# One engine for the branch stage's two-operand steps, and running sums for the pooling means

## The chip, the core and the metric

The kernel runs on one core of a Trainium2 chip. A core has five engines that each work through their own queue of instructions in order: TensorE (PE in the profile; its weight loads are PEld), VectorE (DVE), ScalarE (ACT), GpSimd (POOL) and SyncE (SP), which here issues the loads and stores. TensorE writes to PSUM, in banks; all else lies in SBUF. The metric is the device time of one execution, in microseconds (us).

## The reference

One layer of a decoder trunk on 16 learned meta tokens and 1024 input tokens (L = 1040), width 1024. All is float32.

```
u = rmsnorm(h)
q, f, i, g, v_pool, gate_a, gate_b = split(u @ w_in)
a = hgrn2(q, f, i, g)            # 4 heads of 128: gated linear recurrence, decay per channel
p = multiscale_pool(v_pool)      # 4 groups of 128 channels, windows 2, 4, 8, 16
z = sigmoid(gate_a) * (a @ w_branch_hgrn) + sigmoid(gate_b) * (p @ w_branch_pool)
h = h + rmsnorm(z @ w_out)
u = rmsnorm(h)
y = (gelu(causal_conv3(u @ w_gate)) * (u @ w_up)) @ w_down
out = (h + rmsnorm(y))[16:]
```

The pooling of a group with window w is the mean of the last w values less the value itself, then a 128 x 128 projection:

```
cs0 = cumsum(v, time), with a zero in front
outs = (cs0[t+1] - cs0[t+1-w]) / min(t+1, w) - v[t]
```

In the recurrence, b is the running sum of log f within a chunk, and a pair of times t > s contributes q_t exp(b_t - b_s) k_s.

## The kernel before, in words

Every float32 matrix product is made of three products: each operand is split in a rounded first part and the rest (`hi`, `lo`), and hi x hi, hi x lo and lo x hi are summed. The split of a weight tile (`wsplit`, lines 132 to 139) is a load, a copy on ScalarE that rounds (line 137) and a subtraction that makes the second part (line 138).

The work lies in stages along time: the norm and the value projection, the gates' products (a Strassen scheme), the **branch stage**, the output projection with norms, and the MLP. The branch stage runs from about 285 to 580 us of the profile. It has 34 jobs of projections (F, Q, G, PV, PP, BB, BA: forget logits, queries, output gates, pooling values, pooling projections and the two branch outputs), and between them the steps of the four heads (`h`), the rest of the forget gate (`c`) and the splits of the pooled values and of the heads' outputs (`sp`, `sa`). The list ORDER, line 45, gives the order in which all these are written down. The engines' own order within this stage is not written by hand: a planner, which simulates the engines with a cost model when the kernel is compiled, lays out each engine's queue, in the main by that order. The stages after it have their order fixed for TensorE, ScalarE, VectorE and mostly GpSimd.

A head's steps (`head_steps`, line 578):

- Six levels, of block lengths 2 to 64, taken in three pairs. For each, `level_in` subtracts from b its value at the middle of each block (line 597), takes two exponentials on ScalarE (lines 599, 600) and multiplies one half of every block by q (line 601) and the other by k (line 602), each product over 512 or 520 columns. TensorE makes the small products (lines 613, 619), and VectorE copies them into the scores (lines 633 to 640).
- The decays to the end of a chunk and from its start (lines 654 to 664), a factor on every second q and k (lines 667 to 674), transposes, the states of the eight chunks (line 716), and the output with its norm and gate (lines 725 to 746).

`chain_f` (line 562) makes log f and its running sum b with a scan (line 569). `post_pv` (line 764) copies a pooling group's values from PSUM to `vp` on ScalarE and sums each window by doubling: one addition of shifted copies for window 2, up to four for window 16, all on GpSimd (line 776). `pool_split` (line 780) overwrites the sum of the first kept time for window 16, scales, subtracts `vp` (line 788) and splits the result (lines 793, 794).

Which engine takes a two-operand step is said by the list POOLED: a step named in it goes to GpSimd, all others to VectorE. For example lq8.1 is line 601 of level 8 and head 1, wPV2 the second part of the weights of the job PV2. All tiles of this stage are slots of one ring of 24.

Of the kernel before, what the change touches and what calls it, by code (L numbers as in the profile page):

```python
# [12 lines left out]
ALU = mybir.AluOpType  # L13

P = 128
# [3 lines left out]
L = SEQ + NM  # L19
# [25 lines left out]
ORDER = ("F0 c0 Q0 h0 F1 h0 c1 Q1 h0 h1 F2 h1 c2 h0 Q2 h1 h2 G2 h0 h1 h2 h0 F3 h0 h2 c3 PV0 h1 h2 h1 Q3 h3 h1 "  # L45
         "h3 h1 PV1 h3 sp0 PV2 h2 h3 sa1 sp1 sp2 PP0 h2 PV3 h2 h3 sp3 PP1 h0 G3 h3 PP2 h3 PP3 BB0 h2 BB1 BB2 "
         "sa2 BB3 h3 BB4 BB5 sa0 sa3 BA0 BA1 BB6 BA2 BB7 BA3 BA4 BA5 BA6 BA7")
POOLED = ("e1k.0 e1k.3 kdmul.2 kdmul.3 kdsub.2 lk32.1 lk4.1 lk64.0 lq16.1 lq16.3 lq32.0 lq32.1 lq32.2 lq4.0 "
          "lq64.0 lq64.3 lq8.0 lq8.1 lq8.2 osg.2 qsmul.2 qsmul.3 sub2.2 sub32.1 sub4.1 sub8.1 sub8.3 wBA2 wBA6 "
          "wBA7 wBB2 wF0 wF2 wF3 wPP2 wPV0 wPV1 wPV2 wPV3 wQ0 wQ1 wQ3").split()  # L50
TRUNC = False

CH_ALL = [(0, 348), (348, 346), (694, 346)]
# [4 lines left out]
def trunk_kernel(ctx: ExitStack, tc: tile.TileContext, x, meta_tokens, mix_norm_pre,  # L58
# [4 lines left out]
    act, dve, pool_e, pe = nc.scalar, nc.vector, nc.gpsimd, nc.tensor  # L63
# [21 lines left out]
    def nm(s):  # L85
        cnt[0] += 1
        return f"{s}_{cnt[0]}"

    def slot(n, dtype=F32, name="s"):
        return stage["fm", "p"].tile([P, n], dtype, tag="fm", name=nm(name), padded_shape=[P, L])  # L90
# [65 lines left out]
    def wblock(w, k0, n_k, c0, n_c):  # L156
        return w[k0 * P : (k0 + n_k) * P, c0 : c0 + n_c].rearrange("(k p) c -> p k c", p=P)
# [387 lines left out]
    def blocks(t, lo, h):  # L545
        return t[:, lo:L].rearrange("p (b two h) -> p b two h", two=2, h=h)

    heads = [dict() for _ in range(HEADS)]

    def eng(op):  # L550
        return pool_e if op in POOLED else dve

    sgs = {}

    def post_f(h, pf):
        kk, b, f, f2 = slot(L, name="kk"), slot(L, name="b"), slot(L, name="f"), slot(L, name="f2")
        for (lo, n), ps in zip(CH_ALL, pf):
            act.activation(f[:, lo : lo + n], ps[:, :n], AF.Sigmoid)
            act.activation(kk[:, lo : lo + n], ps[:, :n], AF.Sigmoid, scale=-1.0)
        return lambda: chain_f(h, kk, b, f, f2)  # L560

    def chain_f(h, kk, b, f, f2):
        dve.tensor_scalar(f, f, oml[:, h : h + 1], lb[:, h : h + 1], ALU.mult, ALU.add)
        dve.tensor_scalar(f2, f, LOG_FLOOR, LSPLIT, ALU.max, ALU.min)
        dve.tensor_scalar(f, f, LSPLIT, None, ALU.max)
        act.activation(f2, f2, AF.Ln, scale=LUP)
        act.activation(f, f, AF.Ln)
        eng(f"lf.{h}").tensor_tensor(f, f, f2, ALU.add)
        dve.tensor_tensor_scan(b, again, f, 0.0, ALU.mult, ALU.add)
        heads[h].update(kk=kk, b=b, f=f)  # L570

    def post_q(h, pq):
        q = slot(L, name="q")
        for (lo, n), ps in zip(CH_ALL, pq):
            act.activation(q[:, lo : lo + n], ps[:, :n], AF.Copy, scale=oml[:, h : h + 1])
        heads[h]["q"] = q

    def head_steps(h):
        q, kk, b, lf = (heads[h][z] for z in ("q", "kk", "b", "f"))
# [11 lines left out]
        def level_in(lv):  # L591
            lo = 0 if 2 * lv <= NM else NM
            nb = (L - lo) // (2 * lv)
            d = slot(L, name="d")
            bb, db = blocks(b, lo, lv), blocks(d, lo, lv)
            mid = bb[:, :, 0, lv - 1 : lv]
            eng(f"sub{lv}.{h}").tensor_tensor(db.rearrange("p b two h -> p b (two h)"), bb.rearrange("p b two h -> p b (two h)"),
                              mid.to_broadcast([P, nb, 2 * lv]), ALU.subtract)
            act.activation(db[:, :, 1, :], db[:, :, 1, :], AF.Exp)
            act.activation(db[:, :, 0, :], db[:, :, 0, :], AF.Exp, scale=-1.0)  # L600
            eng(f"lq{lv}.{h}").tensor_tensor(db[:, :, 1, :], db[:, :, 1, :], blocks(q, lo, lv)[:, :, 1, :], ALU.mult)
            eng(f"lk{lv}.{h}").tensor_tensor(db[:, :, 0, :], db[:, :, 0, :], blocks(kk, lo, lv)[:, :, 0, :], ALU.mult)
            return d

        def level_mm(lv, qk):
# [47 lines left out]
        qs, kd = slot(L, name="qs"), slot(L, name="kd")  # L653
        act.activation(qs, b, AF.Exp)
        for t0, n, w in ((0, 1, NM), (NM, NCH, P)):
            bc = b[:, t0 : t0 + n * w].rearrange("p (c t) -> p c t", t=w)
            kc = kd[:, t0 : t0 + n * w].rearrange("p (c t) -> p c t", t=w)
            eng(f"kdsub.{h}").tensor_tensor(kc, bc[:, :, w - 1 : w].to_broadcast([P, n, w]), bc, ALU.subtract)
        act.activation(kd, kd, AF.Exp)
        ebl = small([P, NCH], "ebl", "ebl", 2)  # L660
        act.activation(ebl.rearrange("p (c t) -> p c t", t=1),
                       b[:, NM:L].rearrange("p (c t) -> p c t", t=P)[:, :, P - 1 : P], AF.Exp)
        eng(f"kdmul.{h}").tensor_tensor(kd, kd, kk, ALU.mult)
        eng(f"qsmul.{h}").tensor_tensor(qs, qs, q, ALU.mult)


        e1 = slot(L, name="e1")
# [2 lines left out]
        act.activation(e1[:, L // 2 :], lo2, AF.Exp, scale=-1.0)  # L670
        q2 = q.rearrange("p (b two) -> p b two", two=2)[:, :, 1]
        k2 = kk.rearrange("p (b two) -> p b two", two=2)[:, :, 1]
        eng(f"e1q.{h}").tensor_tensor(q2, q2, e1[:, : L // 2], ALU.mult)
        eng(f"e1k.{h}").tensor_tensor(k2, k2, e1[:, L // 2 :], ALU.mult)
        yield
        kt = slot(NCH * P, name="kt")
        for j in range(2):
# [43 lines left out]
        o, rs = slot(TQ, name="o"), slot(TQ, name="rs")  # L721
# [21 lines left out]
        act.activation(rs, rs, AF.Exp, scale=-0.5)  # L743
        dve.scalar_tensor_tensor(o, o, ong[:, h : h + 1], rs, ALU.mult, ALU.mult)
        sg = sgs[h]
        eng(f"osg.{h}").tensor_tensor(o, o, sg, ALU.mult)
        heads[h] = dict(o=o)

    sgd = dram.tile([EARLY_G, P, TQ], F32, name="gscr")
# [1 line left out]
    def post_g(h, pg):  # L751
        sg = slot(TQ, name="sg")
        for (lo, n), ps in zip(CH_Q, pg):
            act.activation(sg[:, lo : lo + n], ps[:, :n], AF.Sigmoid)
        if h < EARLY_G:
            nc.sync.dma_start(sgd[h], sg)
        else:
            sgs[h] = sg
# [4 lines left out]

    def post_pv(g, pv):
        w = POOL_WINDOWS[g]
        vp, s1 = slot(L, name="vp"), slot(L, name="s1")
        s2 = slot(L, name="s2") if w > 2 else None
        for (lo, n), ps in zip(CH_ALL, pv):
            act.copy(vp[:, lo : lo + n], ps[:, :n])
        cur, step = vp, 1  # L770
        bufs = [s1, s2]
        while step < w:
            nxt = bufs[0]
            bufs = bufs[::-1]
            a = 2 * step - 1
            pool_e.tensor_tensor(nxt[:, a:L], cur[:, a:L], cur[:, a - step : L - step], ALU.add)
            cur, step = nxt, 2 * step
        pooled[g] = (cur, vp)

    def pool_split(g):  # L780
# [16 lines left out]
    def post_pp(g, pp):  # L797
        a, b_ = slot(TQ, F32R, "phi"), slot(TQ, F32R, "plo")
        for (lo, n), ps in zip(CH_Q, pp):
            act.activation(a[:, lo : lo + n], ps[:, :n], AF.Copy, scale=psc[:, g : g + 1])  # L800
            dve.scalar_tensor_tensor(b_[:, lo : lo + n], ps[:, :n], psc[:, g : g + 1], rr(a[:, lo : lo + n]),
                                     ALU.mult, ALU.subtract)
        phi[g], plo[g] = a, b_
# [21 lines left out]
    def post_branch(d, m, qa):  # L825
        for (lo, n), ps in zip(CH_Q, qa):
            dve.tensor_tensor(d[m][:, lo : lo + n], d[m][:, lo : lo + n], ps[:, :n], ALU.mult)
# [11 lines left out]
    def job(kind, i):  # L839
        if kind == "F":  # L840
            return (wblock(WIN, 0, KD, CF + i * P, P), KD, u_all, CH_ALL, lambda r: post_f(i, r))
        if kind == "Q":
            return (wblock(WIN, 0, KD, CQ + i * P, P), KD, u_all, CH_ALL, lambda r: post_q(i, r))
        if kind == "G":
            return (wblock(WIN, 0, KD, CG + i * P, P), KD, u_q, CH_Q, lambda r: post_g(i, r))
        if kind == "PV":
            return (wblock(WIN, 0, KD, CV + i * P, P), KD, u_all, CH_ALL, lambda r: post_pv(i, r))
        if kind == "PP":
            return (pool_proj[0, i].rearrange("(k c) d -> c k d", k=1), 1,
                    lambda k, lo, n: (pin[i][0][:, lo : lo + n], pin[i][1][:, lo : lo + n]), CH_Q,  # L850
                    lambda r: post_pp(i, r))
        if kind == "BA":
            return (wblock(w_branch_hgrn[0], 0, HEADS, i * P, P), HEADS, a_x, CH_Q, lambda r: post_branch(sas, i, r))
        return (wblock(w_branch_pool[0], 0, HEADS, i * P, P), HEADS, p_x, CH_Q, lambda r: post_branch(sbs, i, r))

    order = ORDER.split()
    order = [(o_[:-1], int(o_[-1])) for o_ in order]
# [40 lines left out]
    with tc.manual_schedule(engines={E.Activation, E.DVE, E.PE}):  # L898
# [75 lines left out]
        for e in range(0, EARLY, 2):  # L974
            p = gates.start_pair(e)
# [5 lines left out]
    close_pool("pf")  # L981
    open_pool("ps", 8, PSUM)

    loader = Loader([job(*o_)[:2] + (P, eng("w%s%d" % o_)) for o_ in order if o_[0].isupper()])

    def split_z(c, k):
        zc = slot(2 * CW, F32R, "zc")
# [331 lines left out]
    with tc.manual_schedule(engines={E.PE, E.Activation, E.DVE, E.Pool}):  # L1319
        for c in range(3):  # L1320
            tiles_ = [pair("pm") for _ in range(3)]
            own = Rows(c, tiles_)
            for k in range(KD if c < 2 else KD - 3):
                w = wo.next()
# [45 lines left out]
        p = [ffn.first(e) for e in range(EARLY)]  # L1370
# [171 lines left out]
```

## Time and profile before

| | |
|---|---|
| median of 3 runs | 1375.14 us (1374.52 to 1375.27) |
| the profiled execution | 1376.13 us, its span 1374.4 us |
| granted TensorE clock, mean | 0.991 |
| TensorE busy | 1330.5 us, 97% of the span |
| VectorE busy | 945.2 us, 69% |
| ScalarE busy | 572.9 us, 42% |
| GpSimd busy | 478.8 us, 35% |

The profile records one execution. A busy share is an average over all stages, so a stage is read by itself: the busy time of each engine in a stretch, who waited for whom in it, and the single instructions. In a row of a group of instructions stand the line, the engine, the operation, output and input tiles with their shapes, the count, the busy time in us, the mean duration in ns, and the idle time of the engine in front of them with what ended it. Tile names are those of the program: `d` a level's operand, `sl` its products, `kd` and `qs` the decays, `s` and `vp` the pooling, `whi` and `wlo` the two parts of a weight, `wraw` the weight as it was loaded.

### The profile page before, as it was taken

What the parts mean: (1) busy time and instruction counts of PE and PEld (TensorE: products, weight loads), DVE (VectorE), ACT (ScalarE), POOL (GpSimd) and SP (SyncE); (2) the same over time, 40 slices, a digit from 0 to 9 for tenths busy, and PEclk for the clock granted to TensorE, in tenths of its full rate; (3) what the DMA queues carried; (4) which work ended last, traced back from release to release, by engine and by line L of the source; (5) the groups of instructions that cost most, each with busy time, mean ns of one, the idle gap of its engine ahead of it and who ended that gap; (6) DMA issues with size and microseconds to landing.
All of it is one profiled execution on the core that took longest, in us unless ns stands there. A gap on an engine that the chain in (4) does not pass through costs nothing. (4 is left out here: it accounts for less than half of the span.)

```text
span 1374.4 us, 23322 instructions
## 1 busy us (share of the span) xinstructions
PE 1330.5 (97%) x9375; PEld 1201.1 (87%) x9375; DVE 945.2 (69%) x1213; ACT 572.9 (42%) x965; POOL 478.8 (35%) x371
## 2 busy tenths in 40 slices
PE   9999999998999899999988999999999999999997
PEld 6899999998999899977677888988899998788786
DVE  6764544379877654655689898887888776744557
ACT  5553333366666552135654222232222223643334
POOL 4015421236545410250047565454557642000100
PEclk9999999999999999999999999999999999999999
DMA  7135332311110043698833677756677799965514
GB/s 248 39 101 161 116 112 96 116 48 47 50 50 6 24 139 108 211 291 312 290 116 91 190 209 200 193 175 164 155 162 168 180 233 259 381 218 196 183 62 168
DMA packets 133227, 215.34 MB, mean 157 GB/s; under 512 B 8327, under 2 KB 76523, under 8 KB 133120
## 3 DMA queue, kind: packets, MB, share of 16 engines
q1 hardware_dynamic: 121056, 189.47, 41.4%
q0 software_dynamic: 12064, 24.38, 10.5%
q8 instruction: 74, 1.21, 0.4%
q14 instruction: 33, 0.27, 0.1%
HBM read 160.84 MB, written 76.05 MB: 172 GB/s over the span
## 5 line engine op out<-in xcount | busy, mean ns | idle before, releaser
L263 PE MATMUL P<-v,whi 128*128 128x258 f32 (+2 forms) x528 | 164.2, 325 | 5.2 <-DVE g L1241 3.1
L264 PE MATMUL P<-v,whi 128*128 128x258 f32 (+2 forms) x528 | 162.9, 322 | 0.0
L266 PE MATMUL P<-v,wlo 128*128 128x258 f32 (+2 forms) x528 | 141.4, 322 | 0.4 <-DVE wlo L211 0.4
L138 POOL TENSOR_TENSOR wlo<-wraw,whi 128x1024 fp32r<-128x1024 f32 (+2 forms) x23 | 50.9, 2214 | 180.5 <-ACT whi L137 100.1
L263 PEld LDWEIGHTS P<-v,whi 128*128 128x128 f32 x528 | 101.3, 192 | 13.6 <-DVE g L1241 3.5
L264 PEld LDWEIGHTS P<-v,whi 128*128 128x128 f32 x528 | 101.6, 192 | 7.7
L162 PE MATMUL pd<-rot 128*128 128x512 f32 x272 | 106.0, 390 | 0.3 <-DVE rot L1301 0.3
L163 PE MATMUL pd<-rot 128*128 128x512 f32 x272 | 105.8, 389 | 0.0
L210 ACT CAST whi<-wraw 128x512 fp32r<-128x512 f32 x90 | 53.1, 617 | 104.9 <-PE P L264 85.9
L266 PEld LDWEIGHTS P<-v,wlo 128*128 128x128 f32 x528 | 88.6, 191 | 8.3 <-DVE wlo L211 0.6
L137 ACT CAST whi<-wraw 128x1024 fp32r<-128x1024 f32 (+2 forms) x44 | 36.2, 824 | 128.6 <-PE pba L175 31.3
L1301 DVE TENSOR_TENSOR rot<-yt,rot 128x1024 fp32r<-128x1024 f32 x33 | 41.2, 1250 | 70.4 <-ACT rot L1300 70.4
L211 DVE TENSOR_TENSOR wlo<-wraw,whi 128x512 fp32r<-128x512 f32 x82 | 74.9, 936 | 20.9 <-ACT whi L210 20.9
L1185 POOL TENSOR_TENSOR ys<-y 128x512 f32<-128x512 f32 x22 | 35.3, 1603 | 138.9 <-issue 96.9
L236 POOL TENSOR_TENSOR swa<-wraw,wraw 128x512 f32<-128x512 f32 x30 | 45.6, 1521 | 98.1 <-DMA wraw<-in_w_in_dram 62.7
L161 PE MATMUL pd<-rot 128*128 128x512 f32 x272 | 73.3, 391 | 2.6 <-ACT rot L1300 2.6
L210 ACT CAST whi<-swa 128x512 fp32r<-128x512 f32 x60 | 35.9, 618 | 89.2 <-PE P L264 74.0
L1300 ACT CAST rot<-yt 128x1024 fp32r<-128x1024 f32 x33 | 34.5, 1050 | 88.2 <-PE pd L162 88.2
L1233 DVE SCALAR_TENSOR_TENSOR y<-g,par,y 128x1024 f32<-128x1024 f32 x44 | 65.7, 1494 | 0.7
L161 PEld LDWEIGHTS pd<-rot 128*128 128x128 f32 x272 | 50.8, 188 | 14.2 <-ACT rot L1300 3.7
L210 ACT CAST whi<-swb 128x512 fp32r<-128x512 f32 x60 | 35.9, 619 | 61.0 <-PE P L264 59.5
L211 DVE TENSOR_TENSOR wlo<-swb,whi 128x512 fp32r<-128x512 f32 x60 | 55.1, 923 | 8.6 <-ACT whi L210 8.5
(352 smaller groups left out, 4216.1 us busy)
## 6 DMA issues: line engine op xcount, KB each, us to landing
wraw<-in_w_in_dram SPq DMA_DIRECT2D x36, 512.0 KB
yt<-ysum SPq DMA_DIRECT2D x33, 512.0 KB
wraw<-in_ffn_w_gate_dram SPq DMA_DIRECT2D x26, 512.0 KB
wraw<-in_w_out_dram SPq DMA_DIRECT2D x24, 512.0 KB
wraw<-in_ffn_w_up_dram SPq DMA_DIRECT2D x22, 512.0 KB
wsum<-in_ffn_w_down_dram SPq DMA_DIRECT2D x22, 512.0 KB
ysum<-ys SPq DMA_DIRECT2D x11, 768.0 KB
sa<-sscr SPq DMA_DIRECT2D x16, 513.0 KB
```

The source lines that it names most:

```text
L138: eng.tensor_tensor(lo, raw, rr(hi), ALU.subtract)
L161: pe.matmul(ps, ahi, bhi, start=first, stop=False)
L162: pe.matmul(ps, ahi, blo, start=False, stop=False)
L163: pe.matmul(ps, alo, bhi, start=False, stop=last)
L210: act.copy(hi, src)
L211: (pool_e if 4 <= i < 2 * self.early else dve).tensor_tensor(lo, src, rr(hi), ALU.subtract)
L236: pool_e.tensor_tensor(s1, a21, a22, ALU.add)
L263: pe.matmul(x[:, o : o + w], whi[:, k, :], xh[:, c : c + w], start=(k == 0), stop=False)
L264: pe.matmul(x[:, o : o + w], whi[:, k, :], xl[:, c : c + w], start=False, stop=False)
L266: pe.matmul(x[:, o : o + w], wlo[:, k, :], xh[:, c : c + w], start=False, stop=(k == 3))
L1233: dve.scalar_tensor_tensor(a, g[:, :, j : j + n], cvw[:, j, m : m + 1], a, ALU.mult, ALU.add)
L1301: dve.tensor_tensor(lo, src, rr(hi), ALU.subtract)
```

## The change

The list POOLED and the function that reads it are removed: every step that it could send to GpSimd is on VectorE, and so is the second part of every weight of the branch stage. The doubling sums of the pooling, on GpSimd, become two scans on VectorE for each group: a running sum over the first w times, and from there on a running sum that adds the newest value and subtracts the one that leaves the window. The memsets stay on GpSimd. The kernel's other stages and the order ORDER are as they were.

```diff
-POOLED = ("e1k.0 e1k.3 kdmul.2 kdmul.3 kdsub.2 lk32.1 lk4.1 lk64.0 lq16.1 lq16.3 lq32.0 lq32.1 lq32.2 lq4.0 "
-          "lq64.0 lq64.3 lq8.0 lq8.1 lq8.2 osg.2 qsmul.2 qsmul.3 sub2.2 sub32.1 sub4.1 sub8.1 sub8.3 wBA2 wBA6 "
-          "wBA7 wBB2 wF0 wF2 wF3 wPP2 wPV0 wPV1 wPV2 wPV3 wQ0 wQ1 wQ3").split()
...
-    def eng(op):
-        return pool_e if op in POOLED else dve
...
-            eng(f"sub{lv}.{h}").tensor_tensor(db.rearrange("p b two h -> p b (two h)"), bb.rearrange("p b two h -> p b (two h)"),
+            dve.tensor_tensor(db.rearrange("p b two h -> p b (two h)"), bb.rearrange("p b two h -> p b (two h)"),
                               mid.to_broadcast([P, nb, 2 * lv]), ALU.subtract)
...
-            eng(f"lq{lv}.{h}").tensor_tensor(db[:, :, 1, :], db[:, :, 1, :], blocks(q, lo, lv)[:, :, 1, :], ALU.mult)
-            eng(f"lk{lv}.{h}").tensor_tensor(db[:, :, 0, :], db[:, :, 0, :], blocks(kk, lo, lv)[:, :, 0, :], ALU.mult)
+            dve.tensor_tensor(db[:, :, 1, :], db[:, :, 1, :], blocks(q, lo, lv)[:, :, 1, :], ALU.mult)
+            dve.tensor_tensor(db[:, :, 0, :], db[:, :, 0, :], blocks(kk, lo, lv)[:, :, 0, :], ALU.mult)
...
     def post_pv(g, pv):
         w = POOL_WINDOWS[g]
-        vp, s1 = slot(L, name="vp"), slot(L, name="s1")
-        s2 = slot(L, name="s2") if w > 2 else None
+        vp, cur = slot(L, name="vp"), slot(L, name="cur")
         for (lo, n), ps in zip(CH_ALL, pv):
             act.copy(vp[:, lo : lo + n], ps[:, :n])
-        cur, step = vp, 1
-        bufs = [s1, s2]
-        while step < w:
-            nxt = bufs[0]
-            bufs = bufs[::-1]
-            a = 2 * step - 1
-            pool_e.tensor_tensor(nxt[:, a:L], cur[:, a:L], cur[:, a - step : L - step], ALU.add)
-            cur, step = nxt, 2 * step
+        dve.tensor_tensor_scan(cur[:, :w], vp[:, :w], vp[:, :w], 0.0, ALU.add, ALU.bypass)
+        dve.tensor_tensor_scan(cur[:, w:], vp[:, w:], vp[:, : L - w], cur[:, w - 1 : w], ALU.add, ALU.subtract)
         pooled[g] = (cur, vp)
...
-    loader = Loader([job(*o_)[:2] + (P, eng("w%s%d" % o_)) for o_ in order if o_[0].isupper()])
+    loader = Loader([job(*o_)[:2] + (P,) for o_ in order if o_[0].isupper()])
```

The same replacement of `eng(...)` by `dve` is made at lines 568 (log f), 658, 663 and 664 (decays), 673 and 674 (the factor on every second q and k) and 746 (the output gate).

More of the change, by code (lines that the diff above doesn't have):

```diff
@@ L567, in chain_f @@
         act.activation(f, f, AF.Ln)
-        eng(f"lf.{h}").tensor_tensor(f, f, f2, ALU.add)
+        dve.tensor_tensor(f, f, f2, ALU.add)
         dve.tensor_tensor_scan(b, again, f, 0.0, ALU.mult, ALU.add)
@@ L657, in head_steps @@
             kc = kd[:, t0 : t0 + n * w].rearrange("p (c t) -> p c t", t=w)
-            eng(f"kdsub.{h}").tensor_tensor(kc, bc[:, :, w - 1 : w].to_broadcast([P, n, w]), bc, ALU.subtract)
+            dve.tensor_tensor(kc, bc[:, :, w - 1 : w].to_broadcast([P, n, w]), bc, ALU.subtract)
         act.activation(kd, kd, AF.Exp)
@@ L662, in head_steps @@
                        b[:, NM:L].rearrange("p (c t) -> p c t", t=P)[:, :, P - 1 : P], AF.Exp)
-        eng(f"kdmul.{h}").tensor_tensor(kd, kd, kk, ALU.mult)
-        eng(f"qsmul.{h}").tensor_tensor(qs, qs, q, ALU.mult)
+        dve.tensor_tensor(kd, kd, kk, ALU.mult)
+        dve.tensor_tensor(qs, qs, q, ALU.mult)
         e1 = slot(L, name="e1")
@@ L672, in head_steps @@
         k2 = kk.rearrange("p (b two) -> p b two", two=2)[:, :, 1]
-        eng(f"e1q.{h}").tensor_tensor(q2, q2, e1[:, : L // 2], ALU.mult)
-        eng(f"e1k.{h}").tensor_tensor(k2, k2, e1[:, L // 2 :], ALU.mult)
+        dve.tensor_tensor(q2, q2, e1[:, : L // 2], ALU.mult)
+        dve.tensor_tensor(k2, k2, e1[:, L // 2 :], ALU.mult)
         yield
@@ L745, in head_steps @@
         sg = sgs[h]
-        eng(f"osg.{h}").tensor_tensor(o, o, sg, ALU.mult)
+        dve.tensor_tensor(o, o, sg, ALU.mult)
         heads[h] = dict(o=o)
```

## The prediction

> **What bounds the kernel now.** First the busy times of the whole page:
>
> ```profile
> PE 1330.5 (97%) x9375; PEld 1201.1 (87%) x9375; DVE 945.2 (69%) x1213; ACT 572.9 (42%) x965; POOL 478.8 (35%) x371
> ```
>
> TensorE (PE) is busy for all but 44 us. Its instructions are not touched, so the change can only win or lose the time in which TensorE stands still, or runs at a low clock, because of VectorE (DVE) or GpSimd (POOL). Next the stretches in and around the branch stage. Columns: stretch, its length, busy us of PE, PEld, DVE, ACT, POOL (instructions in brackets), granted clock, DMA share, GB/s.
>
> ```profile
> 240.00:290.00 50.00, 49.84 (x465) 49.30 (x463) 23.05 (x22) 20.26 (x30) 13.23 (x6) 1.00 0.32 94
> 303.20:354.00 50.80, 44.93 (x685) 43.55 (x675) 49.56 (x44) 34.44 (x54) 35.66 (x17) 0.93 0.15 43
> 320.40:325.60 5.20, 5.13 (x181) 4.95 (x182) 4.66 (x10) 4.62 (x6) 2.96 (x2) 0.50 0.35 104
> 354.00:425.00 71.00, 69.44 (x1046) 66.98 (x1044) 47.87 (x75) 46.81 (x80) 27.17 (x17) 1.00 0.14 41
> 425.00:455.70 30.70, 26.31 (x268) 25.34 (x268) 28.70 (x22) 16.57 (x30) 23.79 (x10) 0.99 0.05 14
> 455.70:458.80 3.10, 3.08 (x11) 3.09 (x12) 3.06 (x8) 0.67 (x2) 0.00 (x0) 0.51 0.01 4
> 475.00:580.00 105.00, 105.00 (x670) 103.25 (x669) 60.02 (x93) 36.92 (x57) 10.96 (x8) 1.00 0.41 139
> ```
>
> Before 290 and after 475 TensorE is full and VectorE about half idle; nothing there is waited for. In two stretches, 303 to 354 and 425 to 456, VectorE is full (49.56 of 50.80, 28.70 of 30.70), GpSimd is busy too, and TensorE loses 5.9 and 4.4 us. The waits of TensorE between 285 and 580 name the two places:
>
> ```profile
> PE ppv L174 <- ACT st L707: 4.4, 1, 4.4
> PE sl L619 <- DVE d L602: 4.4, 1, 4.4
> ```
>
> At 316 the first level products wait for a VectorE multiplication (L602). At 451 a pooling projection waits for a PSUM bank that ScalarE has not emptied, because ScalarE's queue stands behind a VectorE step (L788). After each stall the granted clock is about half: 0.50 over 5.20 us and 0.51 over 3.10 us. That is up to 2.6 and 1.5 us more.
>
> Why VectorE is full is seen in single instructions. Four of VectorE, the second of them in the middle of the work of GpSimd that is the fifth row:
>
> ```profile
> 350.40 0.69 DVE L601 TENSOR_TENSOR d<-d,q 128x520 f32<-128x520 f32 x1
> 408.27 3.06 DVE L597 TENSOR_TENSOR d<-b 128x1024 f32<-128x1024 f32 x1
> 358.18 1.22 DVE L664 TENSOR_TENSOR qs<-qs,q 128x1040 f32<-128x1040 f32 x1
> 359.32 1.21 DVE L597 TENSOR_TENSOR d<-b 128x1024 f32<-128x1024 f32 x1
> 408.20 2.04 POOL L597 TENSOR_TENSOR d<-b 128x1040 f32<-128x1040 f32 x1 [3.69 <-PE po L734]
> ```
>
> The same subtraction takes 1.21 us with GpSimd idle and 3.06 us when GpSimd started one 0.07 us earlier. GpSimd's ends at 410.24; 410.24 to the end at 411.33 is 1.09 us, the length of the instruction alone. VectorE did not run slower, it stood still until GpSimd was done. So work on GpSimd here is not beside VectorE's work: it is in series with it, and at 2 us where VectorE alone takes 1.2.
>
> **The change, part by part.** The level steps, decays and weight splits go from GpSimd to VectorE. Durations alone on VectorE: 0.69 for 512 or 520 columns, 1.21 or 1.22 for 1024 to 1040 (rows above). First place, groups of VectorE from 303.2 to 354, then of GpSimd (instructions, busy us and mean ns; idle before):
>
> ```profile
> L602 DVE TENSOR_TENSOR d<-d,kk 128x520 f32<-128x520 f32 (+1 forms) x7 | 13.3, 1893 | 0.0
> L597 DVE TENSOR_TENSOR d<-b 128x1024 f32<-128x1024 f32 (+1 forms) x6 | 12.8, 2169 | 0.0
> L601 DVE TENSOR_TENSOR d<-d,q 128x520 f32<-128x520 f32 (+1 forms) x5 | 8.4, 1684 | 0.0
> L569 DVE TENSOR_TENSOR_SCAN b<-again,f 128x1040 f32<-128x1040 uint8 x2 | 4.7, 2325 | 0.1
> L138 DVE TENSOR_TENSOR wlo<-wraw,whi 128x1024 fp32r<-128x1024 f32 x1 | 2.3, 2323 | 0.0
> ```
>
> ```profile
> L597 POOL TENSOR_TENSOR d<-b 128x1040 f32<-128x1040 f32 (+1 forms) x4 | 10.3, 2566 | 7.0 <-DVE b L569 7.0
> L601 POOL TENSOR_TENSOR d<-d,q 128x512 f32<-128x512 f32 (+1 forms) x5 | 9.0, 1812 | 2.6 <-ACT d L599 2.6
> L138 POOL TENSOR_TENSOR wlo<-wraw,whi 128x1024 fp32r<-128x1024 f32 x3 | 8.4, 2796 | 0.7 <-ACT whi L137 0.7
> L602 POOL TENSOR_TENSOR d<-d,kk 128x512 f32<-128x512 f32 (+1 forms) x3 | 5.7, 1925 | 0.0
> L674 POOL TENSOR_TENSOR kk<-kk,e 128x520 f32<-128x520 f32 x1 | 1.7, 1725 | 11.0 <-DVE kd L663 11.0
> ```
>
> Standing still that goes: L602 13.3 - 7 x 0.69 = 8.5; L597 12.8 - 6 x 1.21 = 5.5; L601 8.4 - 5 x 0.69 = 4.9; L138 2.3 - 1.2 = 1.1; together 20.0 us. Work that comes: 4 x 1.22 + 5 x 0.69 + 3 x 1.22 + 3 x 0.69 + 0.69 = 14.8 us. VectorE is through this stretch 5.2 us earlier although it does everything. TensorE could win 4.4 + 2.6 = 7.0 at most here; VectorE, full from end to end, is what it must wait for, so I take 5.2. If the planner's order puts the later head's subtractions and the weight splits first, as little as 0 is left of it.
>
> Second place, 425 to 455.4, VectorE and then GpSimd:
>
> ```profile
> L597 DVE TENSOR_TENSOR d<-b 128x1024 f32<-128x1024 f32 x2 | 5.5, 2787 | 0.0
> L794 DVE TENSOR_TENSOR pll<-s,plh 128x1026 fp32r<-128x1026 f32 x3 | 4.7, 1585 | 0.0
> L788 DVE SCALAR_TENSOR_TENSOR s<-s,vp 128x1026 f32<-128x1026 f32 x2 | 4.7, 2334 | 0.0
> L794 DVE TENSOR_TENSOR al<-o,ah 128x1026 fp32r<-128x1026 f32 x1 | 3.2, 3211 | 1.3 <-ACT ah L793 1.3
> L658 DVE TENSOR_TENSOR kd<-b 128x16 f32<-128x16 f32 (+1 forms) x2 | 3.0, 1522 | 0.0
> L138 DVE TENSOR_TENSOR wlo<-wraw,whi 128x128 fp32r<-128x128 f32 (+1 forms) x2 | 2.6, 1304 | 0.0
> L601 DVE TENSOR_TENSOR d<-d,q 128x512 f32<-128x512 f32 x1 | 2.4, 2398 | 0.0
> ```
>
> ```profile
> L776 POOL TENSOR_TENSOR s<-s 128x1037 f32<-128x1037 f32 (+1 forms) x3 | 7.5, 2516 | 0.2
> L776 POOL TENSOR_TENSOR s<-vp 128x1039 f32<-128x1039 f32 x2 | 4.9, 2440 | 3.4 <-DVE d L602 3.4
> L663 POOL TENSOR_TENSOR kd<-kd,kk 128x1040 f32<-128x1040 f32 x1 | 3.4, 3413 | 0.0
> L664 POOL TENSOR_TENSOR qs<-qs,q 128x1040 f32<-128x1040 f32 x1 | 2.4, 2440 | 0.0
> L138 POOL TENSOR_TENSOR wlo<-wraw,whi 128x1024 fp32r<-128x1024 f32 x1 | 2.4, 2397 | 11.0 <-ACT whi L137 11.0
> L674 POOL TENSOR_TENSOR kk<-kk,e 128x520 f32<-128x520 f32 x1 | 2.2, 2176 | 0.1
> L601 POOL TENSOR_TENSOR d<-d,q 128x512 f32<-128x512 f32 x1 | 1.7, 1744 | 0.0
> ```
>
> Standing still that goes, at 1.2 alone for each long one and 0.69 for L601 (the small forms of L658 and L138 put at 0.1 and 0.3): 3.1 + 1.0 + 2.3 + 2.0 + 1.7 + 1.1 + 1.7 = 12.9 us. What comes: three long products and splits (L663, L664, L138) 3.7, L674 and L601 1.4, and the pooling sums of two groups. A group's doubling tree (one to four additions on GpSimd) becomes two scans. The long one has the length of L569's, 2.33 us, double an ordinary step; the short one, 2 to 16 columns, has no row: between 0 and the 0.69 of 520 columns, I take 0.2. So 2.5 a group, 5.0 for two, and 10.1 in all. VectorE is 2.8 us earlier; bounds 0 (the scans stand in front of L788) and the whole stall, 4.4. With 4.4 cut to 1.6 I also count the slow clock as gone, 1.5 (bounds 0 and 1.5): from 354 to 425 TensorE stops for 1.6 us in sum, in shorter waits, and the clock stays at 1.00.
>
> Between, 354 to 425, GpSimd's 27.17 us come over at the first place's ratio (14.8 for 35.66, 0.42) as 11.3 us. VectorE has 23 us free there, but it works in order, and a scan or a split in front of a level step can now hold TensorE, which comes earlier and has lost its slack. Bounds 0 and 11.3; I take 1.5, another such sum of small waits as TensorE has there now (71.00 - 69.44).
>
> Nothing is counted for the rest: the splits before 290 and the splits and one gate product after 475 run beside a TensorE that is full (49.84 of 50, 105 of 105), and VectorE has 27 and 45 us free. GpSimd keeps its memsets, now with nothing in front of them. No DMA is moved; the weight loads on SP's queue wait for the splits that free their raw buffers, and no wait of TensorE names a weight. Three groups take one slot of the 24 less; no cost.
>
> Sum: -5.2 - 2.8 - 1.5 + 1.5 = -8.0 us. The profiled execution took 1376.13 us (span 1374.4 and 1.7 around it), so 1368.1 by that one; it is 1.0 above the median of the runs, 1375.14, and the forecast in medians is 1367.1.
>
> [...]
>
> **The rivals.** *VectorE gives it all back* (same): the planner writes the order of each engine anew, and if it puts the 14.8 us early, ahead of the level products, the wait at 316 stays as it is and TensorE's later gains meet the next late step. For it: VectorE is full for 50 us and stays so. Against it: 5.2 us less of it. About 1375.
>
> *The running sums block* (slower): four groups, 2.5 us each, in VectorE's queue, where GpSimd did them aside; each scan also waits for ScalarE's copies, and all behind it waits too. If all four stand in front of a step that TensorE needs and the first place alone gains, 1375.1 - 5.2 + 4 x 2.5 + 1.5 = 1381.4. With a stall and a slow clock a scan costs up to 2.5 + 1.5 = 4.0, so two such scans cancel the forecast's 8.0 and a third makes it slower. For it: the second stall lies in the pooling part. Against it: VectorE has 23 us free in 354 to 425, where two groups fall.
>
> *The long rows are not GpSimd's doing* (slower): then they stay long, and 14.8 us come on top of a full VectorE: 1375.1 + 14.8 - 1.2 (its idle time there) = 1389. The pair at 408 speaks against it.
>
> **How the numbers follow.** The forecast's mechanism 0.63, VectorE gives it back 0.18, the sums block 0.15, long rows stay long 0.04. A difference of 0.2%, 2.75 us, is about what a measurement of this kernel can tell from none. The forecast's own range is 1362 (both stalls and both slow clocks gone: 7.0 + 4.4 + 1.5 = 12.9) to 1372. Faster is the first case, 0.63; same the second, 0.18; slower the last two, 0.19. The range for 8 in 10 leaves the last rival and most of the third out at the top: 1362 to 1379.
>
> **What would show it.** In the changed kernel GpSimd has only memsets from 290 to 575; no subtraction of 1024 columns takes over 1.3 us on VectorE there and no level product over 0.8; VectorE's busy time over the stage changes by a few us only, while GpSimd's 100 go; the waits at L619 and at the pooling projections fall from 4.4 to under 2, and the clock stays at 1.00. It is wrong if VectorE's rows stay long, if TensorE waits at new places for a step behind a scan or a split, or if the branch stage ends earlier and the stage after it, which loads its weights at a high DMA share, waits for these instead.

## The result

The changed kernel takes 1364.51 us in the median (1362.99 to 1365.64), against 1374.83 (1374.20 to 1375.27) for the kernel before beside it: a ratio of 0.9924, with a 95% interval of 0.9912 to 0.9937, or 10.3 us less. The forecast was 8.0 less. The profiled execution took 1364.31 us, with a span of 1362.5, 11.9 less than before. The page's busy times of the changed kernel:

```profile
PE 1324.9 (97%) x9375; PEld 1195.7 (88%) x9375; DVE 941.1 (69%) x1264; ACT 575.2 (42%) x967; POOL 363.3 (27%) x318
```

GpSimd lost 115.5 us of work and VectorE, which took it over, is busy 4.1 us less. TensorE's busy time, for the same 9375 matmuls, fell by 5.6 us, and its idle time (span less busy) from 43.9 to 37.6.

The stretches of the branch stage in the changed kernel (stretch, length, then busy us of PE, PEld, DVE, ACT, POOL, granted clock, DMA share, GB/s):

```profile
303.20:354.00 50.80, 46.56 (x804) 44.80 (x799) 46.99 (x68) 39.66 (x62) 1.26 (x2) 1.00 0.19 55
354.00:425.00 71.00, 69.58 (x918) 67.15 (x917) 51.57 (x82) 46.48 (x78) 1.41 (x4) 1.00 0.11 34
385.00:400.00 15.00, 15.00 (x149) 14.77 (x136) 14.61 (x24) 7.84 (x16) 1.20 (x2) 1.00 0.25 77
425.00:456.00 31.00, 31.00 (x310) 30.06 (x309) 28.90 (x43) 14.75 (x29) 0.00 (x0) 1.00 0.07 20
```

The clock stays at 1.00. In 303 to 354 VectorE carries 68 instructions instead of 44 in 46.99 us instead of 49.56. In 425 to 456 it is about as full as before, and TensorE is busy for all of it: a full VectorE alone does not say that TensorE waits. All of TensorE's waits between 285 and 575:

```profile
PE sb L685 <- DVE kk L668: 1.6, 1, 1.6
PE pq L171 <- ACT kk L553: 1.0, 1, 1.0
PE sl L607 <- ACT kk L553: 1.0, 1, 1.0
PE ms L735 <- ACT rs L731: 0.8, 1, 0.8
PE sl L613 <- issue: 0.8, 1, 0.8
PE ds L707 <- issue: 0.6, 1, 0.6
PE pf L171 <- ACT st L701: 0.6, 1, 0.6
PE pf L171 <- ACT q L569: 0.3, 1, 0.3
```

Both stalls of 4.4 us are gone, and with them the half clock. The longest of the new waits is the first row: the products of a head's nearest pairs wait for the factor on every second k (line 668, line 674 before).

Single kinds of VectorE's instructions from 285 to 575, shapes kept apart (count, busy us, mean ns, idle before):

```profile
L591 DVE TENSOR_TENSOR d<-b 128x1024 f32<-128x1024 f32 x11 | 13.0, 1211 | 0.0
L591 DVE TENSOR_TENSOR d<-b 128x1040 f32<-128x1040 f32 x9 | 10.9, 1232 | 0.0
L595 DVE TENSOR_TENSOR d<-d,q 128x520 f32<-128x520 f32 x10 | 6.9, 694 | 3.6 <-ACT d L593 3.6
L764 DVE TENSOR_TENSOR_SCAN cur<-vp,cur 128x1038 f32<-128x1038 f32 x1 | 2.4, 2380 | 0.1
L763 DVE TENSOR_TENSOR_SCAN cur<-vp 128x2 f32<-128x2 f32 x1 | 0.2, 154 | 0.0
```

The subtraction (line 591, 597 before) takes 1.21 us where its mean was 2.17 in the first place, the product over 520 columns 0.69 where it was 1.68. A pooling group costs 2.5 us, as put in the sum, its short scan 0.15 of it. GpSimd from 285 to 580 has memsets and, at the end, splits of the next stage's weights, the first of them at 565. Two of its rows:

```profile
L135 POOL TENSOR_TENSOR wlo<-wraw,whi 128x1024 fp32r<-128x1024 f32 x3 | 7.2, 2389 | 168.8 <-ACT whi L134 168.8
L579 POOL MEMSET sc<- 128x1024 f32 x2 | 1.9, 949 | 76.9 <-ACT e L664 76.9
```

Where the time came from is read off the starts of TensorE's matmuls. The view of a tile gives the first and last start of each line; for the last branch output (`pba`), before and then changed:

```profile
L178 PE MATMUL pba<-ah,wlo x96: 313/318/334, 528.9 to 584.4; 128*128 128x342 f32 x96
```

```profile
L175 PE MATMUL pba<-ah,wlo x96: 316/319/338, 519.7 to 575.4; 128*128 128x342 f32 x96
```

The same views for the projections F, Q, PV and BA divide the stage into four parts, here from the first start of an F product to the last start of F, from there to the last of Q, of PV, and of BA. The first stall lies in the first part, the second in the third. In us, of the profiled execution of each kernel that ran:

| kernel | to F's last | to Q's last | to PV's last | to BA's last | stage | against before |
|---|---|---|---|---|---|---|
| before | 116.2 | 34.0 | 57.1 | 123.6 | 330.9 | |
| changed | 112.8 | 34.0 | 51.2 | 124.2 | 322.2 | -8.7 |
| dead reads | 138.4 | 35.4 | 57.5 | 124.2 | 355.5 | +24.6 |
| dead memsets | 112.8 | 33.9 | 51.2 | 124.2 | 322.1 | -8.8 |
| scans alone | 116.2 | 36.1 | 54.7 | 123.5 | 330.5 | -0.4 |
| moves alone | 112.8 | 33.9 | 52.5 | 123.9 | 323.1 | -7.8 |
| weights on GpSimd | 112.4 | 34.5 | 51.3 | 123.5 | 321.7 | -9.2 |
| steps on GpSimd | 114.3 | 34.6 | 54.7 | 123.4 | 327.0 | -3.9 |
| more scans | 112.7 | 34.0 | 64.4 | 126.4 | 337.5 | +6.6 |
| no long scans | 112.8 | 34.0 | 51.0 | 123.8 | 321.6 | -9.3 |
| weights, one addition | 112.4 | 34.0 | 51.2 | 123.6 | 321.2 | -9.7 |
| next stage too | 112.8 | 33.9 | 51.2 | 124.2 | 322.1 | -8.8 |

So 3.4 us came from the first part and 5.9 from the third; the last part is 0.6 longer. A further 1.0 came at the seam to the next stage, whose first product started 1.1 us after the last of BA before and 0.1 after it now. Some 2.0 us more lie between that product and the last of the kernel (781.5 before, 779.5 now), where the code is the same.

### The profile page after: what moved, and what is told of

Its sections match the earlier page's. It is cut to its first block, busy times and chain, and to the rows that moved or that the text cites. A ratio compares the mean times of both kernels' runs of the same rounds, so it can differ in the third digit from the quotient of the medians.

```text
span 1362.5 us, 23303 instructions
## 1 busy us (share of the span) xinstructions
PE 1324.9 (97%) x9375; PEld 1195.7 (88%) x9375; DVE 941.1 (69%) x1264; ACT 575.2 (42%) x967; POOL 363.3 (27%) x318
## 3 DMA queue, kind: packets, MB, share of 16 engines
q8 instruction: 74, 1.21, 0.4%
## 5 line engine op out<-in xcount | busy, mean ns | idle before, releaser
L1287 ACT CAST rot<-yt 128x1024 fp32r<-128x1024 f32 x33 | 34.6, 1052 | 89.1 <-PE pd L159 89.1
L135 POOL TENSOR_TENSOR wlo<-wraw,whi 128x1024 fp32r<-128x1024 f32 x8 | 19.2, 2398 | 173.8 <-ACT whi L134 173.8
L260 PE MATMUL P<-t2h,whi 128*128 128x258 f32 (+1 forms) x196 | 57.2, 308 | 4.4 <-ACT t2h L331 2.8
```

The source lines that it names most:

```text
L260: pe.matmul(x[:, o : o + w], whi[:, k, :], xh[:, c : c + w], start=(k == 0), stop=False)
```

## The experiments

My theory: work of GpSimd that reads SBUF stops VectorE's two-input steps for its whole length (3.06 us against 1.21 at 408), and the time came from VectorE being through its queue earlier. Rivals: any work of GpSimd does it; the scans and not the moves bring the gain; the scans cost time that the moves pay for; the weight splits matter, or only the steps of the heads.

### What makes VectorE's rows long

**Dead reads.** In the changed kernel GpSimd makes two subtractions that nobody uses for each level of a head.

```diff
             mid = bb[:, :, 0, lv - 1 : lv]
+            for _ in range(2):
+                pool_e.tensor_tensor(vmeta[64:, :], b[64:, :512], b[64:, 512:1024], ALU.subtract)
```

> The changed kernel and, for each of the 24 levels, two subtractions of 512 columns on GpSimd that read a head's running sum b and whose result nobody uses (48, about 1.3 us each alone, 62 us). Nothing waits for them but GpSimd's own memsets and the slot of b. Theory of exclusion: VectorE's steps with two inputs in SBUF wait for each that is under way; two heads' bursts fall where VectorE is full (12 x 1.3 = 15.6 us for each head), so 15 us or more come on top: 1380 to 1400, and rows of 0.7 and 1.2 us become 1.5 to 3. Rival (GpSimd cost time only as a slow link of the chain): 1364.5.

Measured: 1397.91 us (1396.82 to 1401.38), ratio 1.0164, 1.0149 to 1.0179. VectorE from 303 to 354, then GpSimd from 285 to 600, then TensorE's longest waits, all of this kernel:

```profile
L593 DVE TENSOR_TENSOR d<-b 128x1024 f32<-128x1024 f32 (+1 forms) x9 | 16.0, 1830 | 0.0
L598 DVE TENSOR_TENSOR d<-d,kk 128x512 f32<-128x512 f32 (+1 forms) x6 | 8.2, 1368 | 0.0
L597 DVE TENSOR_TENSOR d<-d,q 128x512 f32<-128x512 f32 (+1 forms) x6 | 8.2, 1362 | 0.0
```

```profile
L592 POOL TENSOR_TENSOR vmeta<-b 64x512 f32<-64x512 f32 x44 | 82.8, 1881 | 41.8 <-DVE b L563 38.6
```

```profile
PE sl L615 <- DVE d L598: 11.8, 4, 4.8
PE sb L687 <- DVE kk L670: 8.4, 1, 8.4
PE pt L677 <- DVE kd L659: 5.1, 1, 5.1
```

The long rows are back, with the same instructions on VectorE as in the changed kernel and in the same order, and so are the waits for it. The planner's order is thus not what makes them long.

**Dead memsets.** The same place, with about as much time on GpSimd, nearly all of which only writes:

```diff
             mid = bb[:, :, 0, lv - 1 : lv]
+            pool_e.tensor_copy(vmeta[64:, 0:1], b[64:, 0:1])
+            for _ in range(5):
+                pool_e.memset(vmeta[64:, :], 0.0)
```

> The changed kernel and, for each of the 24 levels, one copy of one column of b and five memsets of 512 columns on GpSimd, about 0.5 us each, as long together as the reads of the run beside it (some 60 us), in the same places of GpSimd's queue, but reading nothing. If it is the reading of SBUF that excludes VectorE: 1364.5, VectorE's rows as in the changed kernel. If any work on GpSimd does, or if the memsets of the heads behind it in GpSimd's queue are what costs: as slow as the run with reads, 1380 or more.

Measured: 1365.12 us (1363.88 to 1366.44), ratio 0.9925, 0.9908 to 0.9941: as the changed kernel. VectorE from 303 to 354, then GpSimd from 285 to 575:

```profile
L594 DVE TENSOR_TENSOR d<-b 128x1024 f32<-128x1024 f32 (+1 forms) x12 | 14.2, 1221 | 0.0
L598 DVE TENSOR_TENSOR d<-d,q 128x512 f32<-128x512 f32 (+1 forms) x10 | 6.8, 679 | 0.5 <-ACT d L596 0.5
```

```profile
L593 POOL MEMSET vmeta<- 64x512 f32 x108 | 59.5, 551 | 6.2
L591 POOL COPY vmeta<-b 64x1 f32<-64x1 f32 x21 | 18.0, 857 | 26.8 <-DVE b L563 25.6
```

77.5 us of GpSimd's time left VectorE's rows as they are, again in the same order. So it is not GpSimd's time or its queue that stops VectorE, but its subtractions, which read SBUF at full length; an instruction of GpSimd that reads one operand at full length was not tried. The copies of one column hint at the other direction: 0.86 us in the mean for 64 x 1 elements, while a memset of 64 x 512 takes 0.55; they may stand and wait for VectorE, which was not tried by itself. VectorE's subtractions and products with two inputs in SBUF take 1.83 and 1.36 us in the mean beside GpSimd's subtractions, against 1.22 and 0.68 beside its memsets.

### Which part of the change brings the time

**Scans alone**: the kernel before with the pooling sums as scans on VectorE, all else where it was.

```diff
-            pool_e.tensor_tensor(nxt[:, a:L], cur[:, a:L], cur[:, a - step : L - step], ALU.add)
...
+        dve.tensor_tensor_scan(cur[:, :w], vp[:, :w], vp[:, :w], 0.0, ALU.add, ALU.bypass)
+        dve.tensor_tensor_scan(cur[:, w:], vp[:, w:], vp[:, : L - w], cur[:, w - 1 : w], ALU.add, ALU.subtract)
```

> The kernel before with the running sums alone; all other steps stay where the list put them. Theory (a VectorE instruction with two inputs in SBUF and a GpSimd instruction that reads SBUF exclude each other): the first place, 303 to 354, has no pooling additions and stays as before, with its wait of 4 us and its slow clock. In the second place 12.4 us of GpSimd additions go and 5.0 us of scans come, the decay products stay on GpSimd; about half of that place's 5.9 us is won: 1372 (1369 to 1374). Rival (the gain is the shorter way of the level steps, off GpSimd's slow and ordered queue): the sums are no level step, 1375, or slower by the scans.

**Moves alone**: the changed kernel with the doubling sums on GpSimd as before (the same diff turned round).

> The changed kernel with the doubling sums left on GpSimd. Theory of exclusion: the first place gains its 3.5 us and the slow clock as in the changed kernel; beside the additions, 22.5 us of GpSimd between 388 and 472, VectorE stands still again for up to that long where it is busy, so one half of the second place's 5.9 us comes back: 1367.5 (1365 to 1370). Rival of the level steps: all level steps are on VectorE, so 1364.5 as the changed kernel.

Measured: scans alone 1372.30 us (1370.52 to 1373.70), ratio 0.9970, 0.9960 to 0.9981; moves alone 1368.32 (1366.52 to 1370.40), 0.9944, 0.9931 to 0.9956. TensorE's longest waits with the scans alone:

```profile
PE sl L619 <- DVE d L602: 4.4, 1, 4.4
PE ppv L174 <- DVE sc L633: 1.9, 1, 1.9
PE pq L174 <- DVE scm L700: 1.9, 1, 1.9
```

The first stall is untouched, the second is down to 1.9, and a new one of 1.9 stands between the two, so that the stage is only 0.4 us shorter. The medians show more, 4.2 us: in the profile 0.9 of it is the seam to the next stage, and 2.4 lie between the first product of the next stage and the last of the kernel (779.1 against 781.5), where the code is the same; on that, see the end of the next section. The third part gained 2.4 us, about the half of 5.9 that was expected, but the new wait took 2.1 of it back; that the median still came as expected is in part luck. The moves alone bring 7.8 of the stage's 8.7 us; with the sums on GpSimd the third part is 1.3 longer than in the changed kernel, where some 3 were expected. In the medians they bring less, 8.2 of 10.3 us: the profiled execution, 1366.52, was the fastest of the five.

**Weights on GpSimd**: the changed kernel, with the 15 weight splits that GpSimd had before given back to it. **Steps on GpSimd**: the changed kernel with the 27 other steps given back instead.

```diff
+POOLED = "wBA2 wBA6 wBA7 wBB2 wF0 wF2 wF3 wPP2 wPV0 wPV1 wPV2 wPV3 wQ0 wQ1 wQ3".split()
...
-    loader = Loader([job(*o_)[:2] + (P,) for o_ in order if o_[0].isupper()])
+    loader = Loader([job(*o_)[:2] + (P, eng("w%s%d" % o_)) for o_ in order if o_[0].isupper()])
```

> The changed kernel with the 15 weight splits of the list back on GpSimd, level steps, decays and sums on VectorE. No wait of TensorE names a weight. Theory of exclusion: 3 splits fall in the first place and 1 in the second; each stops VectorE for up to 2.4 us and frees 1.2 us of its work, so up to 4 us come back where VectorE is full: 1367 (1365 to 1370), and level steps beside a split last over 1.5 us. Rival of the level steps: the splits are on no chain and VectorE has 1.2 us less for each: 1364.5 or a little less.

> The changed kernel with the 27 level, decay and gate steps of the list back on GpSimd, weight splits and sums on VectorE. Theory of exclusion: GpSimd has some 20 us of level steps in the first place beside a full VectorE, less the 8.4 us of splits: most of the first place's gain is lost, and half of the second's: 1371 (1368 to 1374). Rival of the level steps: all is lost, 1375.

Measured: weights on GpSimd 1365.50 us (1363.55 to 1366.22), ratio 0.9920, 0.9906 to 0.9933, even with the changed kernel; steps on GpSimd 1370.28 (1368.63 to 1371.09), 0.9956, 0.9943 to 0.9968. The splits still stop VectorE, in the timeline of the kernel with the weights on GpSimd (start, length), VectorE and GpSimd:

```profile
345.57 0.68 DVE L600 TENSOR_TENSOR d<-d,kk 128x520 f32<-128x520 f32 x1
346.38 2.79 DVE L599 TENSOR_TENSOR d<-d,q 128x520 f32<-128x520 f32 x1
```

```profile
346.25 2.37 POOL L136 TENSOR_TENSOR wlo<-wraw,whi 128x1024 fp32r<-128x1024 f32 x1 [9.64 <-ACT whi L135]
```

A product of 0.68 us stands until GpSimd's split, begun 0.13 us before it, is over. Yet TensorE does not notice: the first part takes 112.4 us, against 112.8 in the changed kernel. A standing VectorE is not by itself lost time. With the steps on GpSimd both old places are there again, shorter:

```profile
PE sl L617 <- DVE d L600: 2.2, 1, 2.2
PE ppv L172 <- DVE sc L631: 1.9, 1, 1.9
```

It is the steps, then: beside scans on VectorE, moving them takes 8.8 us off the stage (from 330.5 to 321.7) and moving the weights as well 0.5 back on; moving the weights first takes 3.5 off. The two parts don't add: either one shortens VectorE's queue in front of the same waits.

### What the scans cost

**More scans**: four dead scans for each pooling group, on VectorE.

```diff
+        for _ in range(4):
+            dve.tensor_tensor_scan(vmeta[64:, :], vp[64:, :512], vp[64:, 512:1024], 0.0, ALU.add, ALU.bypass)
         pooled[g] = (cur, vp)
```

> The changed kernel and, in each pooling group, four more scans of 512 columns on VectorE whose result nobody uses (about 1.15 us each, 4.7 us a group, 18.7 in all): twice the price of the running sums, at their place. If the sums lie in free time of VectorE, as between 354 and 425, most of it costs nothing: 1364.5 to 1368. If a step in VectorE's queue there holds TensorE, it costs nearly all: up to 1383.

Measured: 1380.25 us (1378.55 to 1381.34), ratio 1.0033, 1.0021 to 1.0044. The dead scans and the longest waits of TensorE in this kernel:

```profile
L766 DVE TENSOR_TENSOR_SCAN vmeta<-vp 64x512 f32<-64x512 f32 x16 | 19.5, 1221 | 0.5
```

```profile
PE ds L707 <- DVE scm L694: 3.2, 1, 3.2
PE sl L613 <- DVE d L596: 2.8, 1, 2.8
PE ms L735 <- DVE scm L694: 2.1, 1, 2.1
```

19.5 us of scans made the stage 15.3 us longer (337.5 against 322.2), though from 354 to 425 VectorE had 19 us free in the changed kernel. The first group's scans do fall in that stretch, at 385, but in its full part: 14.61 of 15 us in the row above; the free part is before and after. The other three come from 429 on. Stretches of this kernel:

```profile
400.00:410.00 10.00, 7.11 (x170) 6.44 (x169) 9.76 (x16) 6.45 (x14) 0.10 (x1) 0.82 0.35 107
433.00:453.00 20.00, 15.81 (x190) 14.80 (x189) 19.57 (x25) 11.11 (x19) 0.00 (x0) 0.86 0.02 5
```

The delay of the first group reaches TensorE right behind that part, and the granted clock falls again where TensorE has stood still.

**No long scans**: the changed kernel with the long scan of each group replaced by a memset on GpSimd.

```diff
-        dve.tensor_tensor_scan(cur[:, w:], vp[:, w:], vp[:, : L - w], cur[:, w - 1 : w], ALU.add, ALU.subtract)
+        pool_e.memset(cur[:, w:], 0.0)
```

> Edit: in the changed kernel the long scan of each pooling group is left out and GpSimd sets those columns to zero instead (it reads nothing), so the sums of the pooling means are left out of the computation and four times 2.3 us = 9.3 us of VectorE's work are gone. The extra scans added 15.4 us to the stage for some 18.7 to 19.5 us of scans, 0.8 us for each. Theory A (every scan costs by that slope, so the four that the change needs cost too): 9.3 x 0.8 = 7.4 us less than the changed kernel, about 0.9870 of the kernel before. Theory B (in the changed kernel the scans lie beside other work: TensorE is busy for all of 425 to 475 at clock 1.00 and waits 1.4 us in sum between 354 and 456, so at most that can be won; the slope of the extra scans holds only past the point at which the slack is used up): 0 to 1.4 us less, ratio 0.991 to 0.9925. I hold B.

Measured: 1364.63 us (1364.18 to 1366.95), ratio 0.9923, 0.9911 to 0.9936: nothing gained. VectorE's work from 425 to 456 falls from 28.90 to 22.70 us, and TensorE is as full as it was:

```profile
425.00:456.00 31.00, 31.00 (x310) 30.08 (x309) 22.70 (x40) 15.75 (x32) 1.92 (x2) 1.00 0.07 20
```

So the same kind of instruction costs nothing when four of it are taken away and 0.8 us per us when sixteen are added. The four that the change needs fit.

**Weights, one addition**: a try for a version that beats both, with the weight splits on GpSimd and the group of window 2 summed by one addition.

```diff
+        if w == 2:
+            dve.tensor_tensor(cur[:, 1:], vp[:, 1:], vp[:, : L - 1], ALU.add)
+        else:
```

> Edit: the changed kernel with the weights' second parts on GpSimd as before, and the group of window 2 summed by one addition of neighbours on VectorE (1.22 us by the rows of an ordinary step) in place of two scans (2.5 us). VectorE is freed of 1.3 us in the pooling part and of the splits. Theory A (each microsecond of VectorE in the branch stage counts): 1 to 3 us faster than the changed kernel, ratio 0.990 to 0.9915. Theory B (what is taken off VectorE there is off the chain, as with the splits alone): even with the changed kernel, 0.991 to 0.9935. I hold B.

Measured: 1365.42 us (1364.21 to 1367.16), ratio 0.9924, 0.9910 to 0.9937. The stage is 1.0 us shorter than in the changed kernel, but 0.6 of that is lost at the seam, where the next stage's first product starts 0.7 us after BA's last instead of 0.1, and the whole time shows nothing of it. No version that beats the changed kernel was found.

### Beyond the stage

**Next stage too**: the differences and sums of the next stage's operands that GpSimd makes go to VectorE as well.

```diff
-        put("b22", c22, d, pool_e)
+        put("b22", c22, d, dve)
...
-        pool_e.tensor_tensor(dst, rr(fq[q + "h"][0][:, :, d]), src, ALU.subtract)
+        dve.tensor_tensor(dst, rr(fq[q + "h"][0][:, :, d]), src, ALU.subtract)
```

> The changed kernel with the same idea one stage on: the steps of the quarters' making (second parts of b22 and t4, and the difference for t4) go from GpSimd to VectorE. They take GpSimd about 20 us between 640 and 770, where VectorE is full from 690 on. By exclusion VectorE would stand still some 8 to 10 us less and have about 9 us more to do: even, with a shorter chain: 1364.5, 1361 to 1368. The rest of GpSimd's work there, weight sums and splits, stays and still excludes.

Measured: 1364.49 us (1363.48 to 1366.72), ratio 0.9919, 0.9904 to 0.9934: even with the changed kernel. Moving these steps brings nothing there; the weight sums and splits, which stayed on GpSimd, were not moved in any run.

## Why the prediction was right, and where its terms were off

The mechanism was right, and is shown: GpSimd's subtractions that read SBUF make VectorE's two-input steps long and its memsets do not (dead reads 1.36 us for a product, dead memsets 0.68), without them the steps take their time alone (1.21 and 0.69 us), and TensorE's two stalls go. Everything listed as what would show it is there: no subtraction of 1024 columns over 1.3 us, no product over 0.8, both waits gone, the clock at 1.00; only the next stage's splits on GpSimd begin at 565, 10 us before I had them. One sign against it shows too, in small: the new wait of 1.6 us for line 668 stands in a queue of VectorE that is full from 336.8 to 348 and holds a weight split and a decay product. With the weight splits on GpSimd this wait is not there. Beside a full VectorE GpSimd was the slower way here: taking its work back gave 10.3 us and did not cost the 13.6 of the last rival.

The sum, -8.0, met -8.7 in the stage and -10.3 in all, with errors in its terms that partly cancelled, so that it came this near is in part luck:

- *First place, -5.2:* it was -3.4. VectorE is indeed earlier and the 4.4 us stall and its slow clock are gone, but TensorE still idles 4.2 us from 303 to 354 (50.80 - 46.56; 5.9 before). The waits there now are for line 668 (1.6), for ScalarE's sigmoid (1.0) and for nothing that the profile shows (0.8 and 0.6). I named no step that would be late next; the sum needed one.
- *Second place, -2.8 - 1.5:* it was -5.9 in the third part, which is the whole stall of 4.4 and the whole slow clock, the upper bound. The step that failed took what VectorE saves over the whole stretch, 2.8, for what TensorE gains, while the wait, of a product of the pooling values (PV), ended with one step: ScalarE's copy `st`, which stood behind VectorE's `pll` (line 794), itself behind the line 788 that the prediction names. Before and changed:

```profile
455.40 0.27 ACT L707 COPY st<-ds 128x128 f32<-128x128 f32 x1 [1.58 <-DVE pll L794]
```

```profile
446.88 0.27 ACT L701 COPY st<-ds 128x128 f32<-128x128 f32 x1 [1.30 <-DVE pll L781]
```

Counted from the last start of a Q product (403.7 and 400.0), it comes after 51.7 us before and 46.9 now, 4.8 earlier: enough for the whole stall. No long scans shows that 6.2 us less of VectorE's work there changes nothing more.
- *Between, +1.5:* it was 0 (34.0 in both), and TensorE's idle time from 354 to 425 is 1.4, as it was 1.6.
- *Nothing before 290 and after 475:* the last part is 0.6 longer, the seam to the next stage 1.0 shorter; the sum had neither.
- *The weight splits* stood in both sums, in the standing still and in the work that comes. They could have been left out: with them on GpSimd the time is the same. That work on GpSimd is in series with VectorE's is shown for GpSimd's subtractions and splits that read SBUF beside VectorE's two-input products (1.36 us in the mean with the dead reads, 2.79 beside a split, 0.68 alone), but TensorE does not wait for all of VectorE's queue.

The rival that the running sums block has a real mechanism (more scans), but a scan has a price, 0.8 us for each us where the rival put 1.0 to 1.6, only past those that the change needs. What I held against it was wrong: I let two groups fall in a stretch with 23 us free; one does, in the full part of it, and the second begins at 424.3, at its end. That VectorE gives it all back is excluded by the two waits; that the long rows are not GpSimd's doing, by the dead reads.

Two things stay open. The planner gave the changed kernel other queues than the kernel before had, and no run holds that order fixed while only the engines change; so how much of the 8.7 us the order itself brings is not known. And the 2.0 us after the branch stage in the profiled execution: the other nine kernels that run the same code there have from 778.9 to 780.9 us between the same two products, so the changed kernel's 779.5 lies among them and the 781.5 before lies 0.6 above; each is a single execution, and no run ties the difference to the change.

## What to carry to other kernels

Before you use GpSimd as a second VectorE, look in the timeline for pairs that start together: if VectorE's instruction ends one length of its own after GpSimd's (1.09 us at 408, alone 1.21), the two are in series, and moving work back to VectorE can make it less busy (941.1 us here, against 945.2). Then price the move by the waits of the engine that sets the end, not by the busy time that is freed: the same 15 splits stop VectorE visibly (2.79 us for a product of 0.68) and cost nothing (ratio 0.9920, against 0.9924 without them on GpSimd). Ask of every stall what is late next, and where in a stretch the free time lies, since added work lands at its own place in the queue and not where the queue is empty.

## What the runs showed of the hardware

That the two engines took turns where both had work queued: with the dead reads VectorE's products of 0.68 us came at 1.76 us each for a while, one for one with GpSimd's subtractions:

```profile
319.17 1.77 DVE L597 TENSOR_TENSOR d<-d,q 128x512 f32<-128x512 f32 x1
320.87 1.76 DVE L598 TENSOR_TENSOR d<-d,kk 128x512 f32<-128x512 f32 x1
```

```profile
310.22 20.26 POOL L592 TENSOR_TENSOR vmeta<-b 64x512 f32<-64x512 f32 x11
```

And how short a wait was enough to slow TensorE, and that its place decided. With the scans alone TensorE waits twice for 1.9 us (rows above), from 392.7 to 394.6 and from 445.7 to 447.6. These are stretches of 3.41 us of that kernel, two with the first wait and one with the second, then the one behind it:

```profile
390.27:393.69 3.42, 2.47 (x18) 2.07 (x18) 3.42 (x1) 2.92 (x4) 3.31 (x2) 1.00 0.07 19
393.69:397.10 3.41, 2.51 (x16) 2.51 (x17) 3.37 (x6) 2.44 (x6) 2.98 (x2) 1.00 0.51 154
444.89:448.30 3.41, 1.52 (x12) 1.36 (x12) 3.37 (x6) 3.41 (x5) 1.12 (x1) 1.00 0.00 0
448.30:451.71 3.41, 3.41 (x14) 3.41 (x13) 3.41 (x2) 2.96 (x5) 2.98 (x2) 0.50 0.02 5
```

The second wait leaves one stretch idle for 1.89 us, and the next runs at half the clock. The first wait is divided, 0.95 and 0.90, and the clock stays at 1.00. The stretches are laid by the half clock's own times: in the kernel before it lasts from 318.81 to 325.63 and from 455.34 to 458.75, two and one times 3.41 us, and the two starts are 136.53 us apart, 40 times 3.413. Later in the kernel with the scans alone 1.76 us of idleness in one stretch were not enough, as the second row's clock shows:

```profile
758.91:762.33 3.42, 1.66 (x7) 1.40 (x8) 3.35 (x4) 1.27 (x3) 3.42 (x3) 1.00 0.26 54
762.33:765.74 3.41, 3.41 (x17) 2.74 (x16) 3.41 (x4) 0.00 (x0) 1.26 (x2) 1.00 1.11 336
```

Laid in this way over the traces of the kernel before and of the changed one, 60 to 1330 us, each from its own half clock, the stretches at the full clock part cleanly: six were followed by half the clock, and the least idle of them was idle for 1.89 us (before, from 724.99); none of the others was idle for more than 1.57 (before, from 752.30). With the 1.76 and the 1.89 of the rows above, the limit in these stretches lies between the two, a little over half a stretch, by TensorE's busy time as the profile models it. Coming back took more: a stretch at half the clock that was idle for 1.35 us was followed by another (changed, from 710.31), one idle for 0.38 by the full clock (before, from 455.34). In the changed kernel the most within one stretch from 285 to 480 is 1.35 (345.08 to 348.50), and the clock stays at 1.00.

So a stall of TensorE can cost more than itself: the second wait above, 1.9 us, was followed by 3.41 us at half the clock, by my estimate up to 1.7 us more.
